# A hybrid decoder layer on one core: a shared PSUM bank and deeper loads in the recurrence, larger key and value weight loads, and two first tiles side by side

## The chip, the cores and the metric

The kernel runs on one core of a Trainium2 chip. The metric is the device time of one execution in microseconds (us). Three executions of the kernel before took 1657.24, 1657.88 and 1666.92 us; their median is 1657.88 us.

## What is computed

One layer of a decoder trunk works on 1024 prompt tokens and 8 x 4 sample tokens (1056 columns in all), with model width 1024 and everything in float32:

```python
h = rmsnorm(x, norm_mix); proj = h @ w_in                # z, xbc, dt, v_pool
xbc = silu(causal_dwconv(conv_buf, xbc))                 # width 4
y = ssd_chunked(xs, dt, a, b_ssm, c_ssm, ssm_h)          # 16 heads, chunks of 128
y = gated_group_rmsnorm(y + xs * ssm_d, z, ssm_norm)
pooled = (window means 2/4/8/16 of v_pool - v_pool) @ w_pool * pool_scale
x = x + concat(y, pooled) @ w_out
k, v = rmsnorm(mem, norm_memkv) @ w_mk, ... @ w_mv       # 256 memory tokens
x = x + attention(rmsnorm(x) @ w_mq, k, v) @ w_mo        # 4 heads
x = x + (silu(g) * val) @ w_down                         # from conv3(rmsnorm(x) @ w_up)
y = rmsnorm(x, final_norm)
```

The prompt's recurrence runs chunk by chunk: for each chunk and head, `exp` of differences of cumulated decays masks `C B^T`, that mask is multiplied with `x dt`, and the state of 128 x 64 is carried on. States, convolution rows, keys and values are outputs too.

## The kernel before, in words

**Tiles.** Activations lie transposed, 128 channels by 1056 tokens. Each float32 product is made of three TensorE products: operands are split into a rounded part (`wh`, `hh`) by ScalarE and a remainder (`wl`, `hl`) by VectorE. `mm_full` (L353) makes one output tile of 128 x 1056 in three PSUM banks: for each of 8 blocks k of 128 channels it issues nine matmuls of 352 columns (three for `wh` with `hh`, three for `wh` with `hl`, three for `wl` with `hh`).

**Weights.** A table of `steps` holds, in the order of use, one unit of 512 weight columns each (256 KB); a unit serves four blocks k. `plains` (L224) enters a unit with a load two steps earlier (`AHEAD`), into the pool `wr` of three buffers, and `wsplit` makes `wh` and `wl` of it (three buffers each). `next_unit` (L299) keeps two units ready ahead of the matmuls.

**Pools.** `stile` gives one of 32 large SBUF tiles (`s`), `ldtile` one of three (`ld`), `mstile` one of two small PSUM banks (`ms`), `mmtile` one of two groups of three banks (`mm`). A new tile takes a buffer when the last user of the old one is done.

**Order.** In the first stage the program's order holds on each engine; later a scheduler orders the instructions of each engine when the kernel is built, and each engine works its list in order. SyncE (SP) issues all loads and stores but a few, also in list order: one that waits holds back those behind it. Generators run beside the matmuls and are advanced by `tick`, one call per block k.

**Start** (L461 to L500, L664 to L672). TensorE first multiplies zeros (`WARM` = 6 instructions, two records each in the trace). `x` arrives in eight blocks `xs[k]`, each split by `x_split(k)` into `hh[k]` and `hl[k]`; the first comes in three pieces. Then two projection tiles are made one after the other, and a third while the norm is found.

**Recurrence** (`ssd_all`, L881). There are 32 units: two groups of heads, eight chunks, two halves of four heads. `ssd_load` (L708) loads 256 KB of cumulated decays (`scr_acs`) into an `s` tile, two units ahead. `ssd_pre` (L715) transposes two blocks of `x` into an `ms` bank, from which VectorE makes `xd`; then ScalarE and VectorE turn the decays into `am` and `ce` in the same `s` tile. `ssd_post` (L741), one unit later, multiplies: the output `py` in one `ms` bank, the new state `pst` in another; VectorE adds both away. All of this lies between the matmuls of the projection tiles.

**Keys and values** (L1060 to L1088). After the pooled half of the output projection (L1047, eight tiles, for each of which `xT` is loaded into an `ld` tile, added and stored), the keys take 8 x 8 blocks of three matmuls of 256 columns, the values 2 x 8 blocks of six matmuls of 512 columns, so that a unit of 256 KB lasts for 12 or for 6 matmuls. The weights `w_mk` and `w_mv` come as 32 such units.

Of the kernel before, what the change touches and what calls it, by code (L numbers as in the profile page):

```python
# [10 lines left out]
ALU = mybir.AluOpType  # L11
# [3 lines left out]
P = 128  # L15
D = 1024
KT = 8
# [6 lines left out]
BW = 352  # L24
TW = 1191
NB = 3
# [2 lines left out]
DFF = 2816  # L29
NJ = DFF // P  # L30
EPS = 1e-6
WARM = 6
XN_TICK = 18
XN_LAG = 6
MEM_EVERY = 1.5
# [1 line left out]
VZ = "ppzppzpzpzpzpzzz"  # L37
SSD_EVERY = 3
SSD_PACE = 1.6
SAMPLE_EVERY = 1.5  # L40
GATE_EVERY = 1.5
FOLD_EVERY = 1.2
WINDOWS = (2, 4, 8, 16)
AHEAD = 2
# [19 lines left out]
XBC_ORDER = (8, 10, 0, 1, 2, 3, 9, 11, 4, 5, 6, 7)  # L64
# [15 lines left out]
def body(ctx, tc, A):  # L80
# [20 lines left out]
    V, S, G, PE, DQ = [InOrder(e) for e in (nc.vector, nc.scalar, nc.gpsimd, nc.tensor, nc.sync)]  # L101
# [3 lines left out]
    def dma(out, in_, after=None):  # L105
        d = DQ.dma_start(out, in_)
        after = after or gate[0]
        if after is not None:
            tc.add_manual_dep(d.ins, after.name, NOSYNC, reason="load order")
        return d  # L110
# [32 lines left out]
    def stile(dt=F32, w=T):  # L143
        return sp.tile([P, w], dt, tag="S", name="s")
# [4 lines left out]
    def ldtile():  # L149
        return lp.tile([P, T], F32, tag="ld", name="ld")  # L150

    def mmtile():
        return pmm[0].tile([P, NB, 512], F32, tag="mm", name="mm")
# [4 lines left out]
    def mstile():  # L158
        if pmm[1] is None:
            return mbtile()  # L160
        return pmm[1].tile([P, 512], F32, tag="ms", name="ms")
# [15 lines left out]
    steps, sources, issue = [], [], {}  # L177
    ready = deque()
    raws = {}
    at = [0]  # L180
# [8 lines left out]
    def load(i):  # L189
        if i in raws:  # L190
            return
        src, alloc = sources[i]
        raw = alloc()
        w = 1
        for d in src.shape[1:]:
            w *= d
        dst = raw[:, :w]
        dma(dst if len(src.shape) == 2 else dst.rearrange("p (k o) -> p k o", k=src.shape[1]), src)
        raws[i] = (raw, w)

    def source(src, step, ahead, alloc=wtile):
        sources.append((src, alloc))
        issue.setdefault(max(0, step - ahead), []).append(len(sources) - 1)
        return len(sources) - 1
# [8 lines left out]
    def wsplit(raw, w):  # L213
        hi = wp.tile([P, 512], F32R, tag="wh", name="wh")
        S.activation(hi[:, :w], raw[:, :w], AF.Copy)
        lo = wp.tile([P, 512], F32R, tag="wl", name="wl")
        V.tensor_tensor(lo[:, :w], raw[:, :w], hi[:, :w].bitcast(F32), op=ALU.subtract)
        ready.append((hi, lo, w))
# [5 lines left out]
    def plains(srcs):  # L224
        for src in srcs:
            i = source(src, len(steps), AHEAD)
            steps.append(lambda i=i: plain(i))

    def up_part(j, n):
        return A["w_up"][2 * j + 2 - int(n[1]), int(n[2]) - 1]  # L230

# [41 lines left out]
    def down_weights(name, m, c):  # L273
        kind = {"t3": 0, "b22": 1, "t1": 2, "t2": 3}
        if name in kind:
# [1 line left out]
        h, r = {"b11": (0, 0), "t4": (1, 1)}[name]  # L277
        return A["w_dn"][h, 4 * r + m][:, c]

    plains(A["w_in"][m, h] for m in range(28) for h in range(2))  # L280
    plains(scr["wop"][4 * h:4 * h + 4, :, m * P:(m + 1) * P].rearrange("k p o -> p k o")
           for m in range(8) for h in range(2))
    plains(A["w_mk"][m][:, h * 512:(h + 1) * 512] for m in range(8) for h in range(2))
    plains(A["w_mv"][4 * d + k // 2][:, (k % 2) * 512:(k % 2) * 512 + 512] for d in range(2) for k in range(8))
    for nm, n in (("w_out_y", 8), ("w_mq", 8), ("w_mo", 8), ("w_mo", 8), ("w_mo", 7)):
        plains(A[nm][m, h] for m in range(n) for h in range(2))
    plains(up_part(j, "a12") for j in EARLY)
# [11 lines left out]
    def next_unit():  # L299
        while len(ready) < 2 and at[0] < len(steps):  # L300
            prep()
        return ready.popleft()
# [14 lines left out]
    def tick():  # L317
        for hk in list(hooks):
            hk[0] -= 1
            if hk[0] <= 0:  # L320
                hooks.remove(hk)
                hk[1]()
        for bs in (bgs, bgs2):
            if bs:
                b = bs[0]
                b[1] += 1
                while b[1] >= b[2]:
                    b[1] -= b[2]
                    if next(b[0], 0) == 0:
                        bs.pop(0)  # L330
                        break
# [21 lines left out]
    def mm_full(nk, xh, xl):  # L353
        ps = mmtile() if pmm[1] else [mbtile() for _ in range(NB)]
        for k in range(nk):
            whi, wlo = next_block()
            for pi, (w, x) in enumerate(((whi, xh[k]), (whi, xl[k]), (wlo, xh[k]))):
                for b in range(NB):
                    PE.matmul(bank(ps, b)[:, :BW], lhsT=w, rhs=x[:, b * BW:(b + 1) * BW],
                              start=(k == 0 and pi == 0), stop=(k == nk - 1 and pi == 2))  # L360
            tick()
        return ps
# [102 lines left out]
    ps = mstile()  # L465
# [6 lines left out]
    for b in range(NB):  # L472
        c = slice(b * BW, (b + 1) * BW)
        dma(xs[0][:, c], A["xT"][0][:, c])
    for k in range(1, 8):
        dma(xs[k][:, :T], A["xT"][k])
        if k in (2, 4):
            load(k // 2)
    dma(cst, A["cst"][:, :256])
    dma(chist, A["conv_hist"])  # L480
    dma(cst2, A["cst"][:, 256:])
# [3 lines left out]
    hh, hl = [], []  # L485
# [10 lines left out]
    prep()  # L496
    for k in range(8):
        x_split(k)
        if k == 2:
            prep()  # L500

    def x_sq(k):
# [86 lines left out]

    xb = [None] * 12  # L590

    def xbc_raw(f):
        ps = mm_full(KT, hh, hl)
        raw = ttile()
        if xr[1:]:
            normed(raw[:, 3:3 + T], ps)
        else:
            S.activation(v3(raw[:, 3:3 + T]), ps[:, :, :BW], AF.Copy)
        return raw
# [64 lines left out]
    later(10, dt_weights)  # L664
    later(XN_TICK, lambda: xr.append(norm_cols(xs[0], T, D)))
    later(XN_TICK + XN_LAG, x_bc)
    early_raw = [xbc_raw(f) for f in XBC_ORDER[:2]]
    strict[0] = "after"
    background(fold_pool(), FOLD_EVERY)
    ps = mm_full(KT, hh, hl)  # L670
# [7 lines left out]
    ps = mmtile()  # L678
    for k in range(KT):
        for pi, x in enumerate((hh[k], hl[k])):  # L680
            for b in range(NB):
                PE.matmul(ps[:2 * H, b, :BW], lhsT=wd[:, k].rearrange("p s h -> p (s h)"),
                          rhs=x[:, b * BW:(b + 1) * BW], start=(k == 0 and pi == 0), stop=(k == KT - 1 and pi == 1))
# [23 lines left out]

    def ssd_load(c, g, hf):  # L708
        h0 = 8 * g + 4 * hf
        at = stile()  # L710
        dma(at[:, 0:512].rearrange("p (h l) -> p h l", h=4),
            scr["acs"][h0:h0 + 4, c * P:(c + 1) * P].partition_broadcast(P))
        return at
# [27 lines left out]
    def ssd_post(c, g, hf, am, ce, xd, btm):  # L741
        l = slice(c * P, (c + 1) * P)
        h0 = 8 * g + 4 * hf
        py = mstile()
        for i in range(2):
            o = slice(i * P, (i + 1) * P)
            for e in range(2):
                PE.matmul(py[64 * e:64 * e + 64, o], lhsT=xd[:, 0, 2 * i + e], rhs=am[:, 2 * i + e],
                          start=True, stop=(c == 0))
            if c > 0:  # L750
                for e in range(2):
                    hc = (h0 + 2 * i + e) * 64
                    PE.matmul(py[64 * e:64 * e + 64, o], lhsT=hT[:, hc:hc + 64], rhs=ce[:, 2 * i + e],
                              start=False, stop=True)
        pst = mstile()
        PE.matmul(pst[:, :256], lhsT=btm, rhs=xd[:, 1].rearrange("p h d -> p (h d)"), start=True, stop=True)
        for i in range(2):
            x = xb[h0 // 2 + i]
            V.scalar_tensor_tensor(x[:, l], x[:, l], pc("ssm_d", h0 // 2 + i), py[:, i * P:(i + 1) * P],
                                   op0=ALU.mult, op1=ALU.add)  # L760
        hs = hT[:, h0 * 64:h0 * 64 + 256]
        if c == 0:
            V.tensor_copy(hs, pst[:, :256])
        else:
            hv = hs.rearrange("p (h d) -> p h d", h=4)
            V.tensor_tensor(hv, hv, cd_t[:, c, h0:h0 + 4].unsqueeze(2).to_broadcast([P, 4, 64]), op=ALU.mult)
            V.tensor_tensor(hs, hs, pst[:, :256], op=ALU.add)
        if c == 7:
            dma(A["o_ssm_p"][:, h0 * 64:h0 * 64 + 256], hs)

# [108 lines left out]
    units = [(c, g, hf) for g in range(2) for c in range(8) for hf in range(2)]  # L879

    def ssd_all():  # L881
        loads = {}
        loads[0] = ssd_load(*units[0])
        loads[1] = ssd_load(*units[1])
        yield
        yield
        pend = None
        for u, un in enumerate(units):
            if un[2] == 0:
                ssd_group(un[0], un[1])  # L890
                yield
            nxt = ssd_pre(*un, loads.pop(u))
            yield
            if pend is not None:
                ssd_post(*pend[0], *pend[1])
            if u + 2 < len(units):
                loads[u + 2] = ssd_load(*units[u + 2])
            yield
            pend = (un, nxt)
        ssd_post(*pend[0], *pend[1])  # L900
        yield
# [145 lines left out]
    for m in range(8):  # L1047
        ps = mm_full(KT, p2h, p2l)
# [11 lines left out]
    for m in range(8):  # L1060
        ps = mbtile()[:, :256]
        for k in range(8):
            whi, wlo = next_block()
# [9 lines left out]
    for d in range(2):  # L1073
        pv = [mbtile() for _ in range(2)]
        for k in range(8):
            whi, wlo, _ = next_unit()
            for mt in range(2):
                c = slice(mt * P, (mt + 1) * P)
# [920 lines left out]
```

## Time and profile before

| | |
|---|---|
| median of three executions | 1657.88 us |
| the profiled execution, its own time | 1659.16 us |
| its span in the profile | 1657.3 us |
| TensorE matmul busy (PE) | 1633.0 us, 99% |
| TensorE weight loads busy (PEld) | 1556.8 us, 94% |
| VectorE (DVE), ScalarE (ACT) busy | 1213.8 us, 73%; 805.2 us, 49% |
| moved by DMA | 287.42 MB, 173 GB/s on average |
| granted TensorE clock, mean | 0.998 |

PE rows are modelled in their ends, so a PE row can run on over a short wait. The weight loads (PEld) have ends of their own, and a wait that PE hides shows there. All instructions go through one recording helper, so the trace tells them apart by the names of their tiles.

### The profile page before, as it was taken

To read this page: it belongs to the slowest core of one execution; us is meant where nothing else is said; L and a number is where in the kernel's file an instruction comes from. 1 tells how busy PE (TensorE), PEld (TensorE's weight loads), DVE (VectorE), ACT (ScalarE), POOL (GpSimd) and SP (SyncE) were. 2 spreads that over 40 slices of the span, in tenths; PEclk is the share of its full clock that TensorE was granted. 3 is DMA by queue.
4 is the path that set the end of the run, shared out by engine and by line. 5 is a ranking of instruction groups with operands and counts; after the bars stand their busy time and mean duration, and the time that the engine had idled before them with its cause. 6 is when DMAs were issued, how large, how long until landed. Compare 5 with 4: busy or idle time off the path is not lost.

```text
span 1657.3 us, 30394 instructions
## 1 busy us (share of the span) xinstructions
PE 1633.0 (99%) x11808; PEld 1556.8 (94%) x11808; DVE 1213.8 (73%) x2044; ACT 805.2 (49%) x1578; POOL 51.5 (3%) x117
## 2 busy tenths in 40 slices
PE   9999999999999999999999999999999999999998
PEld 8899999899989989999888999999999999999997
DVE  7766778688679576754654887888888898866665
ACT  7565643443505342312543666566665656554451
POOL 0110000000000000000000000010000000000000
PEclk9999999999999999999999999999999999999999
DMA  6243354544687578962665654554434356986542
GB/s 222 86 158 92 65 136 105 109 94 100 202 294 269 177 242 302 312 214 72 230 216 191 219 184 120 171 139 119 137 126 146 125 163 196 317 294 191 164 131 105
DMA packets 174592, 287.42 MB, mean 173 GB/s; under 512 B 39936, under 2 KB 77664, under 8 KB 174448
## 3 DMA queue, kind: packets, MB, share of 16 engines
q1 hardware_dynamic: 171584, 281.03, 53.9%
q0 software_dynamic: 2864, 4.46, 1.9%
q8 instruction: 92, 1.51, 0.4%
q14 instruction: 52, 0.43, 0.1%
HBM read 207.89 MB, written 77.53 MB: 172 GB/s over the span
## 4 chain that ended last, share of the span: by engine, by line
PE 74%; DMA 6%; DVE 4%; ACT 1%; issue 1%; SPq 0%; DVEq 0%; ACTq 0%
PE mb L92 59%; PE mm L92 12%; PE ms L92 3%; DMA s<-scr_acs 2%; DVE s L92 2%; DMA q<-scr_g 1%; DVE wl L92 1%; ACT s L92 1%; DMA wr<-w_mk 1%; DMA wr<-w_mo 1%; DVE t L92 0%; DMA scr_pool<-t 0%; DMA ld<-scr_pool 0%; ACT wh L92 0%; DMA wr<-w_up 0%
## 5 line engine op out<-in xcount | busy, mean ns | idle before, releaser
L92 PE MATMUL mb<-s,wh 128*128 128x264 f32 (+4 forms) x4800 | 904.6, 294 | 5.1 <-ACT wh L92 5.1
L92 PEld LDWEIGHTS mb<-s,wh 128*128 128x128 f32 x4800 | 758.4, 189 | 11.9 <-ACT wh L92 6.2
L92 PE MATMUL mb<-s,wl 128*128 128x264 f32 (+4 forms) x2400 | 664.3, 294 | 2.4 <-DVE wl L92 2.3
L92 PEld LDWEIGHTS mb<-s,wl 128*128 128x128 f32 x2400 | 445.4, 189 | 6.9 <-DVE wl L92 4.1
L92 ACT ACTIVATE wh<-wr 128x512 fp32r<-128x512 f32 (+1 forms) x298 | 184.1, 619 | 389.7 <-PE mb L92 181.3
L92 PE MATMUL mm<-s,wh 128*128 128x352 f32 x1728 | 340.8, 330 | 1.0 <-DVE s L92 0.9
L92 PEld LDWEIGHTS mm<-s,wh 128*128 128x128 f32 x1728 | 284.8, 188 | 7.2 <-DVE s L92 2.1
L92 DVE TENSOR_TENSOR wl<-wr,wh 128x512 fp32r<-128x512 f32 (+1 forms) x298 | 201.6, 679 | 112.9 <-ACT wh L92 111.5
L92 PE MATMUL mm<-s,wl 128*128 128x352 f32 x864 | 187.8, 324 | 0.0
L92 DVE SCALAR_TENSOR_TENSOR t<-t,par 128x1104 f32<-128x1104 f32 (+1 forms) x124 | 168.9, 1366 | 19.3 <-ACT t L92 18.5
L92 PEld LDWEIGHTS mm<-s,wl 128*128 128x128 f32 x864 | 147.2, 189 | 1.8 <-issue 1.2
L92 ACT ACTIVATE s<-s 128x512 f32<-128x512 f32 (+7 forms) x117 | 84.2, 731 | 93.4 <-DMA s<-scr_acs 57.4
L92 DVE TENSOR_TENSOR t<-t 128x1024 f32<-128x1024 f32 (+10 forms) x147 | 105.7, 731 | 12.9 <-DMA t<-w_dn 9.7
L92 ACT ACTIVATE wh<-ws 128x512 fp32r<-128x512 f32 x110 | 68.9, 628 | 69.9 <-PE mb L92 67.8
L92 DVE TENSOR_TENSOR s<-s 128x512 f32<-128x512 f32 (+8 forms) x90 | 74.6, 844 | 30.8 <-ACT s L92 30.4
L92 DVE TENSOR_TENSOR wl<-ws,wh 128x512 fp32r<-128x512 f32 x110 | 75.7, 689 | 22.0 <-ACT wh L92 21.7
L92 DVE TENSOR_TENSOR s<-mb,s 128x264 f32<-128x264 f32 (+6 forms) x140 | 61.0, 473 | 31.2 <-PE mb L92 16.3
L92 ACT ACTIVATE t<-mb 128x264 f32<-128x264 f32 (+1 forms) x136 | 53.3, 393 | 57.4 <-PE mb L92 50.3
L92 DVE TENSOR_TENSOR s<-q,s 128x528 fp32r<-128x528 f32 x81 | 56.4, 708 | 25.6 <-ACT s L92 25.4
L92 ACT ACTIVATE t<-t,par 128x1104 f32<-128x1104 f32 (+1 forms) x56 | 73.0, 1304 | 2.3 <-DVE t L92 1.7
L92 ACT ACTIVATE s<-q 128x528 fp32r<-128x528 f32 x81 | 51.9, 643 | 43.0 <-DMA q<-scr_g 41.3
L92 PE MATMUL mb<-s 128*128 128x256 f32 (+2 forms) x414 | 68.8, 323 | 0.0
(195 smaller groups left out, 1427.4 us busy)
## 6 DMA issues: line engine op xcount, KB each, us to landing
q<-scr_g SPq DMA_DIRECT2D x77, 264.0 KB, 4.0
wr<-w_up SPq DMA_DIRECT2D x59, 256.0 KB, 2.9
wr<-w_in SPq DMA_DIRECT2D x56, 256.0 KB, 2.9
wr<-w_mo SPq DMA_DIRECT2D x46, 256.0 KB, 2.8
scr_g<-t SPq DMA_DIRECT2D x22, 528.0 KB, 2.7
ws<-w_up SPq DMA_DIRECT2D x44, 256.0 KB, 2.8
s<-scr_acs SPq DMA_DIRECT2D x33, 256.0 KB, 5.0
t<-w_dn SPq DMA_DIRECT2D x32, 256.0 KB, 4.4
```

What stands on the lines that cost most here:

```text
L92: i = fn(*args, **kwargs)
```

## The change

Four edits are made. (1) `WARM` becomes 3, the two first projection tiles are made side by side for the first four blocks k, and the second tile's first weights are loaded and split earlier. (2) In the recurrence the state `pst` is written to the free half of `py`'s bank. (3) The decays are loaded four units ahead, every second unit into an `ld` tile. (4) The key and value weights are loaded as 16 tiles of 512 KB into `ld` tiles, four steps ahead, and each is split in two halves.

```diff
-WARM = 6
+WARM = 3
+SSD_AHEAD = 4
...
+    def halves(src):
+        i = source(src, len(steps), 2 * AHEAD, ldtile)
+
+        def half(h):
+            load(i)
+            wsplit(raws[i][0][:, h * 512:(h + 1) * 512], 512)
+
+        steps.extend([lambda: half(0), lambda: half(1)])
...
-    plains(A["w_in"][m, h] for m in range(28) for h in range(2))
+    plains(A["w_in"][m, h] for m, h in ((0, 0), (1, 0), (0, 1), (1, 1)))
+    plains(A["w_in"][m, h] for m in range(2, 28) for h in range(2))
...
-    plains(A["w_mk"][m][:, h * 512:(h + 1) * 512] for m in range(8) for h in range(2))
-    plains(A["w_mv"][4 * d + k // 2][:, (k % 2) * 512:(k % 2) * 512 + 512] for d in range(2) for k in range(8))
+    for src in (*(A["w_mk"][m] for m in range(8)), *(A["w_mv"][k] for k in range(8))):
+        halves(src)
...
     for k in range(1, 8):
+        if k in (1, 3):
+            load((k + 1) // 2)
         dma(xs[k][:, :T], A["xT"][k])
-        if k in (2, 4):
-            load(k // 2)
...
         x_split(k)
-        if k == 2:
+        if k in (0, 4):
             prep()
...
+    def two_tiles():
+        ps = [mmtile(), mmtile()]
+        u = [next_unit(), next_unit()]
+        for i, k in [(i, k) for k in range(4) for i in range(2)] + [(i, k) for i in range(2) for k in range(4, 8)]:
+            if k == 4:
+                u[i] = next_unit()
+            whi, wlo, _ = u[i]
+            wc = slice(k % 4 * P, (k % 4 + 1) * P)
+            for pi, (w, x) in enumerate(((whi, hh[k]), (whi, hl[k]), (wlo, hh[k]))):
+                for b in range(NB):
+                    PE.matmul(ps[i][:, b, :BW], lhsT=w[:, wc], rhs=x[:, b * BW:(b + 1) * BW],
+                              start=(k == 0 and pi == 0), stop=(k == 7 and pi == 2))
+            tick()
+            if k == 7:
+                yield ps[i]
...
-    early_raw = [xbc_raw(f) for f in XBC_ORDER[:2]]
+    early_raw = [xbc_raw(f, ps) for f, ps in zip(XBC_ORDER[:2], two_tiles())]
...
-        at = stile()
+        at = ldtile() if (2 * c + hf) % 2 else stile()
...
-        pst = mstile()
-        PE.matmul(pst[:, :256], lhsT=btm, rhs=xd[:, 1].rearrange("p h d -> p (h d)"), start=True, stop=True)
+        pst = py[:, 256:]
+        PE.matmul(pst, lhsT=btm, rhs=xd[:, 1].rearrange("p h d -> p (h d)"), start=True, stop=True)
...
-        loads[0] = ssd_load(*units[0])
-        loads[1] = ssd_load(*units[1])
+        for u in range(SSD_AHEAD):
+            loads[u] = ssd_load(*units[u])
...
-            if u + 2 < len(units):
-                loads[u + 2] = ssd_load(*units[u + 2])
+            if u + SSD_AHEAD < len(units):
+                loads[u + SSD_AHEAD] = ssd_load(*units[u + SSD_AHEAD])
```

In the lists below, numbers behind a name tell one buffer's use from another's. TensorE's list at the start stands before as follows (`s_146`, `s_154`, `s_158` are `hh[0]`, `hh[1]`, `hh[2]`, the numbers one higher `hl`; `wh_142` is the first unit of weights):

```order
L92 MATMUL ms_105<-warm_96 128x512 x6
L92 MATMUL mm_189<-s_146,wh_142 128x352 x3
L92 MATMUL mm_189<-s_147,wh_142 128x352 x3
L92 MATMUL mm_189<-s_146,wl_144 128x352 x3
L92 MATMUL mm_189<-s_154,wh_142 128x352 x3
L92 MATMUL mm_189<-s_155,wh_142 128x352 x3
L92 MATMUL mm_189<-s_154,wl_144 128x352 x3
L92 MATMUL mm_189<-s_158,wh_142 128x352 x3
```

and in the change so (`s_143`, `s_157` are `hh[0]`, `hh[1]`; `mm_192` is the first tile, `mm_193` the second):

```order
L93 MATMUL ms_105<-warm_96 128x512 x3
L93 MATMUL mm_192<-s_143,wh_139 128x352 x3
L93 MATMUL mm_192<-s_144,wh_139 128x352 x3
L93 MATMUL mm_192<-s_143,wl_141 128x352 x3
L93 MATMUL mm_193<-s_143,wh_151 128x352 x3
L93 MATMUL mm_193<-s_144,wh_151 128x352 x3
L93 MATMUL mm_193<-s_143,wl_153 128x352 x3
L93 MATMUL mm_192<-s_157,wh_139 128x352 x3
```

Each block of `x` now serves nine matmuls of either tile before the next block is needed. In the recurrence TensorE's list has, around the end of one unit, before:

```order
L92 MATMUL ms_2141<-s_1882,xd_2017 64x128 x2
L92 MATMUL ms_2141<-s_1882,s_1157 64x128 x2
L92 MATMUL ms_2141<-s_1882,xd_2017 64x128 x2
L92 MATMUL ms_2141<-s_1882,s_1157 64x128 x2
L92 MATMUL ms_2150<-xd_2017,btm_1938 128x256
L92 MATMUL mm_2094<-s_168,wh_1999 128x352 x3
```

and now:

```order
L93 MATMUL ms_2137<-ld_1625,xd_2014 64x128 x2
L93 MATMUL ms_2137<-ld_1625,s_1154 64x128 x2
L93 MATMUL ms_2137<-ld_1625,xd_2014 64x128 x2
L93 MATMUL ms_2137<-ld_1625,s_1154 64x128 x2
L93 MATMUL ms_2137<-xd_2014,btm_1936 128x256
L93 MATMUL mm_2090<-s_165,wh_2091 128x352 x3
```

The state's matmul (`btm`) wrote a bank of its own, `ms_2150`; it now writes that of the output, `ms_2137`, and the decays lie in an `ld` tile. VectorE's list where the last pooled output tile ends and the keys begin stands in the change so (`ld_5233` is the first 512 KB of `w_mk`, `ld_5347` the second; `ld_5498` holds `xT` for the last tile):

```order
L93 TENSOR_TENSOR wl_5510<-ld_5233,wh_5508 128x512
L93 TENSOR_TENSOR ld_5498<-mm_5399,ld_5498 128x1056
L93 TENSOR_TENSOR wl_5532<-ld_5347,wh_5530 128x512
L93 TENSOR_TENSOR wl_5553<-ld_5347,wh_5551 128x512
L93 TENSOR_TENSOR t_5548<-mb_5507,rmb_4490 128x256
```

`ld_5498` takes the buffer of `ld_5233`, so its load waits for the first row here, and the second row waits for that load; before, `xT` was loaded there without such a tie. Behind the keys and values the lists of all engines are the same as before, row for row, but for line numbers and buffer numbers.

## Rows read from the trace of the kernel before

**Rows 1.** Three stretches: us, then busy us of PE, PEld, DVE, ACT, POOL, clock, DMA, GB/s.
```profile
8.26:33.12 24.86, 24.43 (x147) 23.32 (x145) 19.58 (x19) 19.38 (x21) 0.70 (x3) 1.00 0.74 266
205.00:420.00 215.00, 210.13 (x1531) 196.29 (x1530) 166.06 (x355) 87.69 (x158) 5.55 (x18) 1.00 0.50 109
550.95:603.64 52.69, 49.92 (x309) 42.49 (x308) 35.60 (x59) 24.41 (x38) 0.00 (x0) 1.00 0.63 198
```
**Rows 2.** Timeline of TensorE at the start: start, us, what, count, idle before.
```profile
5.07 0.34 PEld L92 LDWEIGHTS ms<-warm 128*128 128x128 f32 x1 [0.52 <-issue]
5.68 0.19 PEld L92 LDWEIGHTS ms<-warm 128*128 128x128 f32 x1 [0.28 <-issue]
8.26 0.19 PEld L92 LDWEIGHTS mm<-s,wh 128*128 128x128 f32 x1 [0.24 <-issue]
...
28.76 1.13 PE L92 MATMUL mm<-s,wh 128*128 128x352 f32 x6
...
33.12 1.13 PE L92 MATMUL mm<-s,wh 128*128 128x352 f32 x6
```
**Rows 3.** Timeline of ScalarE and VectorE at the start: the splits of x.
```profile
6.55 0.59 ACT L92 ACTIVATE s<-s,par 128x352 fp32r<-128x352 f32 x1 [0.73 <-DMA s<-xT]
7.17 0.58 DVE L92 SCALAR_TENSOR_TENSOR s<-s,par 128x352 fp32r<-128x352 f32 x1 [0.73 <-ACT s L92]
8.31 1.18 ACT L92 ACTIVATE s<-s,par 128x1056 fp32r<-128x1056 f32 x1 [1.17 <-DMA s<-xT]
9.52 2.66 DVE L92 SCALAR_TENSOR_TENSOR s<-s,par 128x1056 fp32r<-128x1056 f32 x2 [1.76 <-ACT s L92]
```
**Rows 4.** Waits of PE, PEld, ACT, SP, 205 to 420: us, times, longest.
```profile
PE ms L92 <- DVE xd L92: 4.3, 6, 1.4
PEld ms L92 <- DVE xd L92: 5.9, 7, 1.6
ACT s L92 <- DMA s<-scr_acs: 59.0, 23, 4.9
SPq L92 <- PE ms L92: 39.2, 20, 3.4
```
**Rows 5.** The chain of waits around one unit: start, us, what.
```profile
292.42 6.17 DMA s<-scr_acs
...
300.63 0.70 PE ms L92 x2
```
**Rows 6.** Waits of PEld, 550 to 604, keys and values.
```profile
PEld mb L92 <- DVE wl L92: 3.7, 8, 1.0
PEld mb L92 <- ACT wh L92: 2.7, 3, 1.4
```
**Rows 7.** Timeline of TensorE, unhindered pieces of keys, transposes and values.
```profile
551.35 0.28 PE L92 MATMUL mb<-s,wl 128*128 128x256 f32 x1
...
561.01 0.28 PE L92 MATMUL mb<-s,wl 128*128 128x256 f32 x1
...
588.83 1.20 PE L92 MATMUL mb<-cst,nr 128*128 128x128 f32 x9
...
591.92 0.39 PE L92 MATMUL mb<-wl,s 128*128 128x512 f32 x1
592.62 0.39 PE L92 MATMUL mb<-wl,s 128*128 128x512 f32 x1
```
**Rows 8.** Timeline: a late weight load, and VectorE's other work late in the values.
```profile
561.81 1.97 ACT L92 ACTIVATE wh<-wr 128x512 fp32r<-128x512 f32 x3 [2.76 <-DMA wr<-w_mk]
...
597.74 1.29 DVE L92 TENSOR_TENSOR wl<-wr,wh 128x512 fp32r<-128x512 f32 x2
598.48 0.19 PEld L92 LDWEIGHTS mb<-wl,s 128*128 128x128 f32 x1 [1.00 <-DVE wl L92]
```
**Rows 9.** DMA issues by line: count, KB each, median us to landing.
```profile
wr<-w_mk SPq DMA_DIRECT2D x16, 256.0 KB, 3.2
ld<-xT SPq DMA_DIRECT2D x8, 528.0 KB, 4.9
```

More of the change, by code (lines that the diff above doesn't have):

```diff
@@ L590, in body, with xbc_raw @@
     xb = [None] * 12
-    def xbc_raw(f):
-        ps = mm_full(KT, hh, hl)
+    def two_tiles():
[13 more added lines that the diff above has]
+                yield ps[i]
+    def xbc_raw(f, ps=None):
+        ps = ps or mm_full(KT, hh, hl)
         raw = ttile()
@@ L762, in ssd_post @@
         if c == 0:
-            V.tensor_copy(hs, pst[:, :256])
+            V.tensor_copy(hs, pst)
         else:
@@ L766, in ssd_post @@
             V.tensor_tensor(hv, hv, cd_t[:, c, h0:h0 + 4].unsqueeze(2).to_broadcast([P, 4, 64]), op=ALU.mult)
-            V.tensor_tensor(hs, hs, pst[:, :256], op=ALU.add)
+            V.tensor_tensor(hs, hs, pst, op=ALU.add)
         if c == 7:
```

## The prediction

> **What bounds the kernel now.** I first read the three stretches that the change touches [rows 1]: TensorE is busy for nearly all of each, at a clock granted in full, while VectorE, ScalarE and the DMA queues have room. So TensorE sets the time, and only what it idles can be won: a transfer or a split that becomes quicker counts as far as TensorE waits for it. Next come the waits of TensorE and of its weight loads in each stretch [rows 4, 6], since a PE row can run on over a short wait and a PEld row cannot; then the timelines around those waits for what came late [rows 2, 3, 8], and the chain of waits for the recurrence [rows 5]. Behind the values the lists of all engines are the same as before, so a gain made ahead of them is carried to the end unchanged if nothing there depends on absolute times; I count it in full.
>
> **The start.** Two tiles take 16 groups of nine matmuls. Unhindered, three groups take 33.12 - 28.76 = 4.36 us, 1.45 each [rows 2], so 16 take 23.2. They took 24.86 us [rows 1], from 8.26: 1.6 us of waiting for x, behind a warm-up that ended late. The warm-up's records stand 0.86 us apart up to 5.68, and from there 0.43 apart [rows 2]. Half of its twelve records go; the six that are left end at about 5.7. The first tile can begin there but needs the last third of `hh[0]` at 6.55 + 0.59 = 7.14 and of `hl[0]` at 7.17 + 0.58 = 7.75 [rows 3]. Four more matmuls (0.16 each) end the first group at about 8.4. The second group, the second tile's, needs its weights. Their load now stands right behind the first block of x; it is half as large as the second block of x, which took from 6.5 to 8.3 to come in [rows 3], so I estimate that it lands 0.8 us after 6.5; both splits (0.65 each, as in [rows 8]) are done at 8.6 to 8.8, before its last three matmuls want the remainder, so the second group ends at 9.9. The second block of x comes 0.8 us later than before, at 9.1; its parts take 1.18 on ScalarE and 1.33 on VectorE [rows 3], so `hh[1]` is there at 10.3 and `hl[1]` at 11.6. The third group thus ends at 11.6 + 6 x 0.16 = 12.6. After that each block of x feeds 2.9 us of matmuls and VectorE needs 1.33 for one, so nothing waits: 13 groups x 1.45 bring the third tile's start to 31.4 instead of 33.12. That is **-1.7 us**. Bounds: with no wait but the first, 8.4 + 15 x 1.45 = 30.2, so -2.9; if x comes one block later than I think (1.7 us), 0.
>
> **The recurrence.** ScalarE waited for decays 23 times, 59.0 us in all [rows 4]. The chain shows how that reached TensorE [rows 5]: the load issued at 292.42 took 6.17 us, ScalarE and VectorE came after, and the state's matmul started at 300.63. That matmul needed an `ms` bank which the transposes held until VectorE had made `xd`, and in VectorE's list `xd` stood behind the late decays. Two edits hit the same wait: the state no longer takes a bank, and the loads go out four units ahead. A unit lasts about 215 / 32 = 6.7 us by the stretch [rows 1] (it holds a few units less, so rather more); two more units are over 13 us against a landing of about 6. TensorE waited 4.3 us for `xd`, its weight loads 5.9 [rows 4]. I take **-4.5 us**, near the PE row, because seven waits of PEld hold the short pause that stands before every state matmul as well. Bounds: -5.9 and, if half of the waits move to the next use of a bank, -2. ScalarE, busy 87.69 of 215 us, covers two more table loads that the new order brings. The `ld` tiles were idle here but for early loads of the sample's state and of `pooled`, which now go out after the last decays; they are needed only behind 425 us.
>
> **Keys and values.** Unhindered, a block of the keys takes (561.01 - 551.35) / 27 = 0.358 us and 64 take 22.9; three value matmuls take 592.62 - 591.92 = 0.70, and 32 such triples 22.4; two sets of transposes for a norm take 1.2 each [rows 7]. Sum 47.7, against 52.69 [rows 1]: 5.0 us lost. The waits of PEld say 6.4 [rows 6], the PE row 2.8 (52.69 - 49.92). Most of it are late weights: a load of 256 KB lands after 3.2 us [rows 9], plus two splits of 0.65, and three buffers of 1.43 us each (four blocks) last 4.3 us, which is no reserve; ScalarE waited 2.76 us for one [rows 8]. With 512 KB tiles three buffers last 8.6 us. The nearest row for such a load is `xT` with 528 KB, 4.9 us [rows 9]; with the splits 6.2, so about 2 us of reserve. Two losses stay. Late in the values VectorE has the gate's work in front of the remainders: a wait of 1.0 us at 598.48 has no load behind it but VectorE's own list [rows 8]; I leave 1.1 us for this. And at the seam to the keys `xT` for the last tile can be loaded only when the first 512 KB are split, in mid tile: that is about 5.8 (half a tile) + 1.3 + 4.9 = 12.0 us after the tile's start, while TensorE ends it at 11.6. VectorE then adds it (about 1.3) and splits the next half unit at about 14.0; TensorE wants that after two units, at 14.5. That holds narrowly, and the fourth 512 KB, behind the store in SP's list, come about 0.5 us late. So 5.0 - 1.1 - 0.5: **-3.4 us**. Bounds: -5.0, and 0 if the seam eats it up. Sixteen issues fewer cost SP less; it waits anyway.
>
> **Sum.** -1.7 - 4.5 - 3.4 = -9.6 us. The profiled execution took 1659.16 us, so its like would take 1649.6; the median lies 1.3 below the profiled time, so I predict a median of **1648.3 us**, 0.6% less. A change of under 1% (16.6 us) is what a measurement of this kernel can hardly tell from none: its own three runs lie 0.6% apart.
>
> **Rivals.**
> *The seam starves the keys* (0.15). The three `ld` buffers now serve x, the keys' weights and the stores of `scr_xp`. If the load of the last `xT` takes 8 us instead of 4.9, VectorE stands still in front of it, the next remainders come 3 us late, and the whole reserve of the following loads starts from there. The gain of 3.4 is gone: 1651.7. For it: one list, one blocked row. Against it: the DMA share of the stretch was 0.63 [rows 1].
> *The clock* (0.07). TensorE ran its first records at 0.86 us and later ones at 0.43 [rows 2], the 1.2 and 2.4 GHz levels, having been at work since its first one. With half of the warm-up gone, real work starts just after the rise and has gaps until 11.6. If the clock fell back in them, the groups up to 12.6 would take 2.9 us instead of 1.45; two of them lie on the path, so +2.9 and the start gains nothing: 1650 to 1651. The Trainium skill, "TensorE: Matmul & The Clock Gate", section "Why this matters for your kernels", speaks against this edit, since it advises to warm the engine with matmuls before work that is measured; by it the sum would be the one just given. The rows decide otherwise as far as they go: the rise stands at 5.68, before the shortened warm-up ends.
> *The shared bank makes VectorE late* (0.06). VectorE reads the output from the bank that the state's matmul now writes, so it starts after that matmul, at most 0.70 us later [rows 5], in each of 32 units. Where VectorE is what TensorE waits for, at seven places [rows 4], up to 4.9 us come back: 1653.2; more only if VectorE, busy 166.06 of 215 us [rows 1], were at its limit. The Trainium skill, "PSUM — Partial Sum Buffer", section "PSUM bank collisions raise a hardware error", states the rule behind it: engines must be kept apart by bank and quadrant, not by address. No row of before shows it.
> *The loads do not go out earlier* (0.06). An `s` buffer is still free only when the unit two `s` units back is done. Then the wait for decays stays, and only the bank's part is won: about half, 1650.5.
> *SP holds back the weights* (0.03; slower). SP works its list in order, and a load of decays waits in it for a buffer that TensorE frees. SP already waited 39.2 us for that, at most 3.4 at once [rows 4]. If the four outstanding loads make it stand longer, the weight loads behind it come late. The splits are two units of weights ahead of the matmuls, each 4 x 1.45 = 5.8 us, so it decides from about 12 us at one stand; if 12 of 24 loads went 2 us over it, the gain of the recurrence would turn into 24 us: 1677. The longest wait is far from it.
> *More than I count* (0.05): waits that PE rows hide, all three bounds at once, -13.8, and something behind: 1640 to 1644.
>
> **Numbers.** The forecast itself has 0.58, and lies between 1645 and 1652. With the rivals on either side the range for 8 times in 10 is **1643.5 to 1654.5**. Faster by over 1% needs less than 1641.3: 0.04. Slower by over 1%: the SP rival, 0.03. Within 1%: 0.93.
>
> **What the changed profile would show.** Start: the third tile's first matmul at about 31.4, records at 0.43 from the sixth on. Recurrence: no TensorE wait for `xd` above 0.5 us, ScalarE's wait for `scr_acs` under 10 us. Keys and values: about 49 us from their first matmul to the first of the next product, ScalarE hardly waiting for `w_mk` and `w_mv`. Wrong I would be through a wait at the seam, in SP's list, or late in the values that is longer than before.

## The result and the profile after

The changed kernel takes **1646.59 us** (median of four runs, 1644.07 to 1649.91); the kernel before, run beside it, 1660.79 us (1657.24 to 1666.92). The ratio is **0.9912**, 95% interval 0.9893 to 0.9931. Measured twice more, the change took 1645.43 us, ratio 0.9901 [0.9869, 0.9933], and 1646.34 us, 0.9892 [0.9873, 0.9911]; the kernel before had medians of 1662.10 (25 runs) and 1662.86 us (17 runs) beside it. So the change is worth 14 to 17 us where I said 9.6, and the time came out 1.7 to 2.9 us below the forecast of 1648.3: the gain was larger than I thought, and so was the time it is taken from.

The profiled execution took 1645.04 us, its span is 1642.9, against 1657.3 before. Four matmuls of TensorE's timeline cut the span into stretches; they are, in order, the third tile's first, the first output of the recurrence, the first of the keys, and the first of the next product (start, length, what):

```profile
32.44 1.13 PE L93 MATMUL mm<-s,wh 128*128 128x352 f32 x6
...
160.43 0.66 PE L93 MATMUL ms<-s,xd 128*64 128x128 f32 x8
...
544.94 0.40 PE L93 MATMUL mb<-s,wh 128*128 128x256 f32 x2
...
592.00 1.13 PE L93 MATMUL mb<-s,wh 128*128 128x352 f32 x6
```

Before, the first is at 33.12 [rows 2]; the others are, in the same view of the kernel before:

```profile
161.08 0.66 PE L92 MATMUL ms<-s,xd 128*64 128x128 f32 x8
...
551.11 0.40 PE L92 MATMUL mb<-s,wh 128*128 128x256 f32 x2
...
603.64 1.13 PE L92 MATMUL mb<-s,wh 128*128 128x352 f32 x6
```

The start is 0.7 us shorter, the stretch with the recurrence 390.0 - 384.5 = 5.5, keys and values 52.5 - 47.1 = 5.5, and what follows 1053.7 - 1050.9 = 2.8, though its lists are the same: 14.4 in all. The stretches of [rows 1], in the same view after (us, then busy us of PE, PEld, DVE, ACT, POOL, granted clock, DMA share, GB/s):

```profile
5.69:32.44 26.75, 24.83 (x146) 23.28 (x145) 21.00 (x22) 20.46 (x23) 2.18 (x3) 1.00 0.78 286
205.00:420.00 215.00, 214.34 (x1564) 201.33 (x1563) 164.10 (x350) 80.93 (x145) 5.57 (x18) 1.00 0.49 112
544.94:592.00 47.06, 47.06 (x308) 42.81 (x307) 36.35 (x59) 24.35 (x39) 0.00 (x0) 1.00 0.70 224
```

TensorE is now busy in all of the last and nearly all of the second; the clock is granted in full throughout, as before. The waits that answer to [rows 4, 6] (us in total, times, longest; the first five from 205 to 420, the others in keys and values):

```profile
PE ms L93 <- DVE xd L93: 0.7, 1, 0.7
PEld ms L93 <- DVE xd L93: 1.4, 3, 0.9
ACT ld L93 <- DMA ld<-scr_acs: 44.4, 11, 4.9
ACT s L93 <- DMA s<-scr_acs: 21.7, 10, 3.5
SPq L93 <- PE ms L93: 57.6, 21, 4.3
...
PEld mb L93 <- issue: 0.2, 1, 0.2
ACT wh L93 <- DMA ld<-w_mk: 1.5, 1, 1.5
```

The reader is to see two things: TensorE's waits are gone, and ScalarE's waits for decays are not. They were 59.0 us and are 66.1.

### The profile page after: what moved, and what is told of

It is laid out like the page before. It is cut to its first block, busy times and chain, and to the rows that moved or that the text cites. A ratio compares the mean times of both kernels' runs of the same rounds, so it can differ in the third digit from the quotient of the medians.

```text
span 1642.9 us, 30318 instructions
## 1 busy us (share of the span) xinstructions
PE 1624.7 (99%) x11802; PEld 1553.6 (95%) x11802; DVE 1214.1 (74%) x2044; ACT 806.9 (49%) x1580; POOL 54.2 (3%) x117
## 4 chain that ended last, share of the span: by engine, by line
PE 89%; DMA 5%; DVE 4%; ACT 1%; issue 1%; SPq 0%; ACTq 0%; DVEq 0%
PE mb L93 60%; PE mm L93 22%; PE ms L93 6%; DVE s L93 2%; DMA q<-scr_g 2%; DVE wl L93 1%; ACT s L93 1%; DMA ld<-scr_pool 1%; DVE t L93 0%; DMA s<-xT 0%; SPq L93 0%; DMA ld<-scr_acs 0%; DMA t<-scr_z 0%; DMA ld<-h0T 0%; DMA wr<-scr_dn 0%
## 5 line engine op out<-in xcount | busy, mean ns | idle before, releaser
L93 ACT ACTIVATE wh<-wr 128x512 fp32r<-128x512 f32 (+1 forms) x266 | 164.2, 618 | 365.6 <-PE mb L93 170.1
L93 DVE TENSOR_TENSOR wl<-wr,wh 128x512 fp32r<-128x512 f32 (+1 forms) x266 | 178.8, 673 | 103.0 <-ACT wh L93 101.4
L93 ACT ACTIVATE s<-s 128x512 f32<-128x512 f32 (+7 forms) x87 | 65.1, 764 | 31.4 <-DMA s<-scr_acs 21.7
L93 DVE TENSOR_TENSOR s<-s 128x528 fp32r<-128x528 f32 (+8 forms) x76 | 64.5, 867 | 6.8 <-ACT s L93 6.3
```

The source lines that it names most:

```text
L93: i = fn(*args, **kwargs)
```

## Experiments

Medians are compared only between kernels that were measured together, on one chip and beside the same runs of the kernel before. One profile shows one execution, so I also read the same stretches from all fourteen. "Units" is the time from the first to the last state matmul (`btm`) of the 32 units of the recurrence, "keys" the time from the first key matmul to the first of the next product, "rest" from there to the end of the span; us:

```
kernel                       third tile  units   keys   rest
before                          33.12    253.7   52.5   1053.7
e3 loads of 512 KB alone        34.08    258.3   47.1   1052.0
e7 short warm-up alone          33.59    257.6   51.0   1052.0
f2 start alone                  32.28    258.0   51.4   1053.3
e2 four units ahead alone       34.11    256.6   53.0   1049.1
e1 shared bank alone            33.80    250.5   51.7   1052.7
f1 change, two units ahead      32.25    251.5   47.1   1052.8
change (after, e4, f3)    31.58..32.44   248.0..248.4   47.1..47.5   1050.9..1053.3
e8 change, 256 KB loads         31.48    249.1   47.1   1052.7
e5 change, x earlier            30.86    249.2   47.1   1053.8
e6, f4 change, long warm-up  32.83, 32.27  249.2, 248.0  47.1  1049.2, 1054.0
```

**e1: the shared bank alone**, in the kernel before.

```diff
-        pst = mstile()
+        pst = py[:, 256:]
...
```

> The kernel before with one edit: the state's product is written to the free half of the output's bank; decays are still loaded two units ahead. Measured by the stretch from the first output matmul of the recurrence to the first matmul of the keys, 389.9 us before and 384.5 in the change (5.4 gained). Theory: late decays and the bank that the transposes hold are one wait, and taking the bank away lets TensorE run on into the projection matmuls while xd is late, so most comes from this alone: 385 to 387 us, TensorE's wait for xd under 1.5 us, while ScalarE still waits some 50 us for decays. Rival, the loads carry the gain: 389 to 390 us, the wait moves to the next transposes or outputs. Rival, each edit has its own half: 387 to 388. Whole kernel: 3 to 5 us less than before by the theory, 0 to 1 by the first rival.

1658.26 us (10 runs) against 1662.10, ratio 0.9978 [0.9964, 0.9991]. Its profile is its quickest run (1655.20). The stretch of the theory takes 386.9 us there, within the 385 to 387 expected; the units take 250.5 us, and TensorE's wait for `xd` from 205 to 420 is down to this, a little over the 1.5 expected, while ScalarE still waits 69.5 us for decays:

```profile
PE ms L92 <- DVE xd L92: 1.9, 3, 1.3
```

**e2: four units ahead alone**, in the kernel before.

```diff
+SSD_AHEAD = 4
...
-        at = stile()
+        at = ldtile() if (2 * c + hf) % 2 else stile()
...
```

> The kernel before with one edit: decays loaded four units ahead, every second unit into an ld tile; the state keeps a bank of its own. Theory (one wait, two cures): with the decays on time xd is on time and the bank is free when the state's matmul wants it, so this alone also brings the stretch from 389.9 to 384.5 to 386 us, and ScalarE's wait for decays falls from 59 us to under 15. Rival, the bank carries the gain: 388 to 390 us although ScalarE waits little. Rival, the loads do not go out earlier since s buffers are still freed late: ScalarE still waits over 40 us for decays.

1658.78 us (10 runs), ratio 0.9979 [0.9963, 0.9994]. The theory fell: the waits of the same stretch are no smaller than in the kernel before:

```profile
PE ms L93 <- DVE xd L93: 6.7, 5, 2.4
...
ACT ld L93 <- DMA ld<-scr_acs: 51.3, 11, 5.8
ACT s L93 <- DMA s<-scr_acs: 15.4, 9, 3.6
```

Where the 3.3 us of its median come from, its profile does not show: the units take 256.6 us, as long as in kernels with two units ahead (253.7 to 258.3), and only the rest, which the edit does not touch, is short.

**e3: the 512 KB loads alone**, in the kernel before.

```diff
...
-    plains(A["w_mk"][m][:, h * 512:(h + 1) * 512] ...)
-    plains(A["w_mv"][4 * d + k // 2][:, ...] ...)
+    for src in (*(A["w_mk"][m] for m in range(8)), *(A["w_mv"][k] for k in range(8))):
+        halves(src)
```

> The kernel before with one edit: key and value weights in 512 KB ld tiles four steps ahead. The stretch of keys and values took 52.7 us before and 47.1 in the change. Theory: the gain of 5.6 us is this edit's alone, so 47.0 to 47.6 us here, no wait of the weight loads over 0.5 us, and the whole kernel is 5 to 6 us shorter than before. Rival, part of it comes from the earlier stages (the seam or VectorE's list stands better because of them): 48.5 to 50.5 us.

1657.85 us (10 runs), ratio 0.9975 [0.9962, 0.9988]: 4.2 us less. Keys and values take 47.05 us, as in the whole change, so the theory holds. Its recurrence, that of before, took 4.6 us longer than in the profile of before. One place shows how (e3, timeline of VectorE, then of TensorE):

```profile
221.69 0.69 DVE L92 TENSOR_TENSOR s<-s 128x512 f32<-128x512 f32 x1 [5.36 <-ACT s L92]
222.30 0.68 DVE L92 TENSOR_TENSOR xd<-ms,dtp 128x512 f32<-128x512 f32 x1
...
223.04 0.70 PE L92 MATMUL ms<-xd,btm 128*128 128x256 f32 x2 [2.38 <-DVE xd L92]
```

It is the mechanism of [rows 5]: VectorE stands 5.36 us in front of late decays, `xd` behind them comes late, and the state's matmul waits for the bank. How often and how long differs from profile to profile.

**e4: the change once more**, unaltered.

> The change itself once more, for the scatter of one program. From the first x1 matmul behind the values to the end both programs have the same lists, yet that part took 1053.7 us before and 1050.9 in the change's first profile. Theory: these 2.8 us are scatter of late weight loads, so the same part takes 1050 to 1055 us here, and differs by up to 3 us among this call's four profiles without regard to the edits. Rival, the change shortens the rest too: 1050 to 1051.5 us here and some 1053.5 in the three kernels that lack parts of it.

1645.43 us (four runs), ratio 0.9901 [0.9869, 0.9933]. The rest takes 1051.8 us here and 1052.7, 1049.1 and 1052.0 in e1, e2 and e3: it scatters without regard to the edits, as the theory has it.

**e5: the change, with x earlier.** Of the first two units of weights only the first 128 columns go ahead of x's second block, and of `par` only eight columns ahead of all. The third unit's load and the splits of what is left move back too.

```diff
...
-    dma(par, A["par"])
-    load(0)
+    dma(par[:, :8], A["par"][:, :8])
+    first_load(0, ca)                      # ca: the first 128 columns
...
+        if k == 1:
+            first_load(1, ca)
+        if k == 2:
+            first_load(0, cb)              # cb: the rest
+            first_load(1, cb)
...
```

> The change with a shorter way to the second block of x: of the parameters only the eight columns of the first norm are loaded ahead, and of the first two weight units only the 128 columns of the first block; the rest follows behind the second block of x. That takes some 0.55 MB out of what is ahead of it. Theory: the start is bound by the second block of x (its two splits ended at 11.07 and 12.43 us, and TensorE stood still from 10.0 to 12.5 but for three matmuls), so the third tile begins at 30.8 to 31.5 us instead of 32.44, and the kernel is 1 to 1.6 us shorter than the change. Rival, the weights' splits or the order on VectorE bind next: 32 to 32.5, nothing won.

The third tile starts at 30.86, about 1 us before the change's own (31.58 to 32.44). The time is 1649.95 us (four runs), ratio 0.9912 [0.9883, 0.9940], no better than the change. TensorE waits in e5 (from 36 to 161, and from 420 to 545 us) where the change has waits of at most 0.5:

```profile
PE ms L93 <- DVE nsu L93: 0.8, 1, 0.8
...
PE ms L93 <- DVE rbc L93: 1.5, 1, 1.5
```

The first goes with a real loss: from the third tile to the first output of the recurrence e5 takes 129.25 us, the change (after, e4, f3) 127.98 to 128.02, so the microsecond was given back by 161 us. That the later load of `par` causes it was not tried. The second is not the edit's: e8, which starts as the change does, waits 1.4 us at the same place.

**e6 and f4: the change with the long warm-up**, with one run and with four.

```diff
-WARM = 3
+WARM = 6
```

> The change with the long warm-up of before (six instructions instead of three). Theory: TensorE waits for the second block of x in any case, so starting at 8.3 instead of 5.7 costs nothing: the third tile begins at 32.3 to 32.6 as in the change (32.44). Rival, the warm-up is what the start gained: 33.1 or later.

> The change with the whole warm-up of before (six instead of three matmuls). Theory: the first real matmul comes at 8.3 instead of 5.7, the wait for x's second block is hidden behind it, and the third tile starts about 1 us later (32.6 to 33.0), so the median is about 1 us above that of the change. Rival: the third tile's start is set by x's arrival alone, which the warm-up doesn't touch; then there is no difference, and half a warm-up was no part of the gain.

e6 took 1644.97 us (one run); f4 1645.83 us (four runs) beside 1646.34 of the change, ratios 0.9891 and 0.9892 to the kernel before. The third tile starts at 32.83 and 32.27. 32.83 lies in the range of f4's theory, 32.27 on its rival's side, and the medians differ by 0.5 us, the long warm-up being the faster. So the shorter warm-up shows no gain, as f4's rival has it; but the 1 us of the theory is less than the intervals, some 3 us to either side, can tell.

**e7: the short warm-up alone**, in the kernel before.

> The kernel before with the short warm-up and nothing else. Theory: one tile takes 1.45 us for each block of x, which comes every 1.4 us, so it waits for x to the last block and the third tile begins at 32.7 to 33.2 us (33.12 before). Rival, the warm-up is what the start gained: 32.4 or earlier. Rival, the clock falls back in the gaps: 34 us or later, and matmuls of 352 columns at about twice their 0.16 us.

1660.13 us (one run) beside 1663.22; the third tile at 33.59 is later than the 32.7 to 33.2 expected and lies within the 33.12 to 34.11 of the kernels with the start of before. The rival of the clock does not show either: behind the longest idle time, 0.93 us, three matmuls take 0.76 us, in the change 0.75.

**e8: the change, but each 512 KB tile filled by two loads of 256 KB.**

```diff
...
+            dma(dst[:, :512], src[:, :512])
+            dma(dst[:, 512:], src[:, 512:])
...
```

> The change with each 512 KB tile of key and value weights filled by two loads of 256 KB, issued one behind the other. Theory: the gain of the keys and values comes from six half units of buffer in place of three, not from larger transfers, so the stretch stays at 47.0 to 47.6 us. Rival, larger transfers and sixteen issues fewer carry it: 49 us or more, with waits for w_mk or w_mv on ScalarE.

1648.46 us (one run). Keys and values take 47.05 us, as with whole loads. Loads of keys and values in e8 and in the change (count, KB each, median us to landing):

```profile
ld<-w_mv SPq DMA_DIRECT2D x16, 256.0 KB, 3.6
ld<-w_mk SPq DMA_DIRECT2D x12, 256.0 KB, 3.5
```
```profile
ld<-w_mv SPq DMA_DIRECT2D x8, 512.0 KB, 4.0
ld<-w_mk SPq DMA_DIRECT2D x6, 512.0 KB, 4.4
ld<-xT SPq DMA_DIRECT2D x1, 528.0 KB, 3.3
```

What counts is that three tiles of 512 KB stand ready instead of three of 256 KB, not the size of a load. The larger tiles and the longer lead (four steps instead of two) were not tried apart.

**f1: the change without the four units ahead.** After e2 I held the loads ahead for worthless.

```diff
-SSD_AHEAD = 4
+SSD_AHEAD = 2
...
-        at = ldtile() if (2 * c + hf) % 2 else stile()
+        at = stile()
```

> The change without its loads four units ahead: the decays go out two units ahead, all into s tiles, as before; the shared bank, the two tiles side by side and the 512 KB loads stay. Theory: the shared bank alone won the recurrence, and the multiplications by the decays moved forward in VectorE's list together with their loads, so nothing waits less. Then the stretch from the first output matmul of the recurrence to the first key matmul takes 385 to 388 us as in the whole change, and the median is within 2 us of that of the change in this call. Rival: the loads ahead are worth the 3.3 us by which the kernel with them alone lay below the kernel before. Then the stretch takes about 389 us and the median is 3 us above that of the change.

1651.85 us (six runs), ratio 0.9927 [0.9911, 0.9942], beside 1646.34 and 0.9892 of the change: 5.5 us. The stretch of the theory takes 388.2 us, in the change (f3) 384.1. My theory fell, and the rival had even too small a price. The waits for `xd` of TensorE and its weight loads (205 to 420 us) and VectorE's longest (165 to 420), of f1 and then of the change beside it (f3):

```profile
PE ms L93 <- DVE xd L93: 2.8, 3, 1.5
PEld ms L93 <- DVE xd L93: 4.2, 5, 1.7
...
DVE s L93 <- ACT s L93: 43.7, 21, 4.7
```
```profile
PE ms L93 <- DVE xd L93: 0.3, 1, 0.3
PEld ms L93 <- DVE xd L93: 0.8, 2, 0.6
...
DVE ld L93 <- ACT ld L93: 23.1, 8, 4.4
```

With two units ahead VectorE waits for decays 21 times, with four 8 times in the units whose decays lie in `ld` tiles, and twice, 1.2 us, in the others. ScalarE's own wait for decays is the same in both, 70.1 and 71.7 us (165 to 420). The sum of the unit spacings falls from 251.5 to 248.0 us, the even pace of 8.0 and 7.6 us in turn that every profile with both edits shows, but for one unit in some. The profile of f1 is its quickest run (1650.34), so 3.5 is what it shows of 5.5.

**f2: the start alone**, in the kernel before (all edits to the first two tiles, and the short warm-up).

> The kernel before with the start of the change alone: three matmuls of warm-up, weights of the first two units loaded early, two tiles side by side. Theory: it is worth what the third tile's first matmul shows between kernels with and without it, about 1.9 us (31.5 to 32.4 against 33.1 to 34.1), so a ratio of 0.999 to the kernel before. Rival: the parts tried alone gave 3.6, 3.3 and 4.1 us, the whole change 15 to 16; if parts simply add, the start has to give the other 4 to 5 us, ratio 0.997, and it would have to show behind the third tile.

1661.20 us (12 runs) against 1662.86, ratio 0.9982 [0.9969, 0.9995]. The interval holds the theory's 0.999 and the rival's 0.997; the profile speaks for the theory, with the third tile at 32.28 and no gain behind it. What part of it the side-by-side order and the earlier weights have was not tried apart. By the medians the parts alone give 3.8 (e1), 3.3 (e2), 4.2 (e3) and 1.7 us (f2), 13.0 in all, and the loads ahead give 5.5 instead of 3.3 once the bank is shared; that makes 15.2 of the 16.5. Each of these parts is uncertain by about 2 us to either side, so whether they simply add is not shown.

**f3: the change, beside f1, f2 and f4.**

> The change itself, timed in the same call as the other three. Every theory expects 1645 to 1648 us and a ratio of 0.990 to 0.992. Its profile shows the scatter of the stretches: third tile's first matmul at 31.4 to 32.5, recurrence to first key matmul 384 to 387 us, keys and values 47.0 to 47.6 us, from there to the end 1049 to 1054 us.

1646.34 us (five runs), ratio 0.9892 [0.9873, 0.9911]; all stretches as expected.

## Why the prediction was right or wrong

**The start (-1.7): right, as a mean.** The profile after shows only 0.7, but both sides scatter. The four profiles with the old start (before, e1, e2, e3) have the third tile at 33.12 to 34.11, mean 33.8; the six with the new one (after, e4, e8, f1, f2, f3) at 31.48 to 32.44, mean 32.0: 1.8 us, and f2's medians say 1.7. Where the profile after lost its 1.0 against my 31.4, its timelines show (ScalarE, VectorE, TensorE; the last bracket is the idle time before and what ended it):

```profile
9.89 1.18 ACT L93 ACTIVATE s<-s,par 128x1056 fp32r<-128x1056 f32 x1 [2.17 <-DMA s<-xT]
...
11.10 2.66 DVE L93 SCALAR_TENSOR_TENSOR s<-s,par 128x1056 fp32r<-128x1056 f32 x2 [2.65 <-ACT s L93]
...
11.12 0.75 PE L93 MATMUL mm<-s,wh 128*128 128x352 f32 x3 [1.08 <-ACT s L93]
12.47 0.75 PE L93 MATMUL mm<-s,wh 128*128 128x352 f32 x3 [0.60 <-DVE s L93]
```

x's second block came at 9.89 where I had 9.1; `hh[1]` and `hl[1]`, and the two waits that I placed in front of them, follow from it, and nothing waits after. Half of this term's story was idle: as far as f4 and e7 can tell, the warm-up could have stayed as it was.

**The recurrence (-4.5): right mechanism, too small.** In the two profiles the units take 253.7 and 248.4 us, 5.3 less. But the kernel before was lucky there: three other profiles with its recurrence (e3, e7, f2) take 257.6 to 258.3; in e7 and f2 all engines have the same lists in that stretch. The mean of the four is 256.9, that of the seven with both edits (after, e4, f3, e5, e6, e8, f4) 248.5: 8.4 us. The step that failed is that I read the term, and its bound of 5.9, off the waits of one execution. A wait that hangs on when a load lands differs from run to run, and the edit takes away the bad runs too.

That no wait for `xd` would be above 0.5 us is nearly so: there is one of 0.7, and one of 1.3 to 1.5 in e5, e6 and e8. That ScalarE would wait under 10 us for decays was wrong. In the change a load goes out 46.7 us before its unit's state matmul instead of 23.9 (medians of the 11th to 30th unit), but ScalarE's and VectorE's work on it moved forward in their lists as well, so both still stand in front of loads in flight (after; ScalarE, VectorE, TensorE):

```profile
297.42 0.63 ACT L93 ACTIVATE ld<-ld 128x512 f32<-128x512 f32 x1 [4.13 <-DMA ld<-scr_acs]
...
298.09 0.69 DVE L93 TENSOR_TENSOR ld<-ld,s 128x512 f32<-128x512 f32 x1 [4.07 <-ACT ld L93]
298.70 0.68 DVE L93 TENSOR_TENSOR xd<-ms,dtp 128x512 f32<-128x512 f32 x1
...
299.44 0.33 PE L93 MATMUL ms<-cst,s 128*128 128x128 f32 x1 [0.66 <-DVE xd L93]
```

The wait of 4.13 us is no shorter than those of before (59.0 us in 23 times, [rows 4]); what reaches TensorE is 0.66. My rival that the loads do not go out earlier had the sign of ScalarE's wait right, the cause and the conclusion wrong: f1 shows that the loads ahead are worth 5.5 us beside the shared bank. The rival of the bank acts, but at no price: from 165 to 420 us VectorE waits for the state's matmul 12 times, 2.3 us in all, where before it never did, but TensorE's wait for VectorE is down to the 0.7 us shown above.

**Keys and values (-3.4): right mechanism, too small by 1 to 1.5.** Profiles without the new loads take 51.0 to 53.0 us (before, e1, e2, e7, f2; mean 51.9), with them 47.05 to 47.5: 4.4 to 4.9 us on the mean, 5.5 between the two profiles. What was missed is partly in the loss, since the stretch without waits takes 47.05 us where I had 47.7, and partly in the two losses that I left in the sum and that are not there. VectorE's gate work is still in front of the remainders late in the values, but each is done ahead of its first weight load, by 0.3 us at the narrowest and 3.2 at the most, and TensorE's stretch has no wait, neither in the change nor in e3. And at the seam (after; VectorE, then SP's issue of `xT`):

```profile
539.50 0.69 DVE L93 TENSOR_TENSOR wl<-ld,wh 128x512 fp32r<-128x512 f32 x1 [0.38 <-ACT wh L93]
545.14 1.26 DVE L93 TENSOR_TENSOR ld<-mm,ld 128x1056 f32<-128x1056 f32 x1 [4.95 <-PE mm L93]
546.32 0.68 DVE L93 TENSOR_TENSOR wl<-ld,wh 128x512 fp32r<-128x512 f32 x1
```
```profile
540.22 0.33 SPq L93 DMA_DIRECT2D ld<-xT  x1
```

`xT` was asked for at 540.22 and took 3.3 us, not 4.9; VectorE waited for TensorE's tile, not for the load. The rival of the seam had no place to act.

**What follows (0): right, but for scatter.** The 2.8 us behind the values are no gain: over fourteen profiles of one and the same program there the rest takes 1049.1 to 1054.0 us, with no relation to what is ahead of it.

**The clock, and SP's list.** TensorE's weight loads tell its level in the profile after (start, length, what):

```profile
5.07 0.34 PEld L93 LDWEIGHTS ms<-warm 128*128 128x128 f32 x1 [0.52 <-issue]
5.66 0.19 PEld L93 LDWEIGHTS mm<-s,wh 128*128 128x128 f32 x1 [0.26 <-ACT s L93]
...
11.12 0.46 PEld L93 LDWEIGHTS mm<-s,wh 128*128 128x128 f32 x3 [1.37 <-ACT s L93]
```

One takes 0.34 us in the warm-up and 0.19 from 5.66 on, where the rise stands before as well [rows 2]; behind the longest gap three take 0.46, so the engine stayed at the upper level; the clock is granted at 1.00 from 5.69 to 32.44. That row alone would not tell: it says 1.00 from 4.20 to 5.10 too, where the records still stand 0.86 us apart. SP's wait for TensorE's `ms` did become longer, which I had named as a sign of being wrong: 57.6 us and at most 4.3, against 39.2 and 3.4 [rows 4]. It comes with the loads ahead (57.3 in e2, 17.5 in f1), stays far from the 12 us from which I let it count, and between 205 and 420 us no split waits for a load of weights. Neither rival came about.

**The sum.** Corrected by the means over the profiles it reads -1.8 for the start, -8.4 for the recurrence and -4.8 for keys and values: -15.0, against 14 to 17 measured. I also started from a median of 1657.88 us of three runs; with more runs the four medians of the kernel before lie at 1660.8 to 1663.2. The low start of 3 to 5 us and the gain that was 5 to 7 too small partly cancelled: that the forecast came within 3 us was luck in part.

## What to carry to other kernels

A wait that comes from a load landing late is not one number: read it in several executions before pricing its removal, because the one profiled may be a good one. Two edits against the same wait can hide each other: in the profiles the deeper prefetch cut TensorE's wait for `xd` only once the matmul no longer needed the bank that the late work held (2.8 to 0.3 us from f1 to f3, but 6.7 in e2). The times, 5.5 us with the shared bank and 3.3 without, point the same way but lie within their intervals. If work on the prefetched data moves forward in the engines' lists with the load, the waits stay in the profile, and only those of the bounding engine tell whether anything was won.

## What the runs showed that I had not expected

A load of 512 KB landed in 4.0 to 4.4 us, one of 256 KB into the same tiles in 3.5 to 3.6: twice the data for 0.4 to 0.9 us more. In e8 the small loads go out in pairs; in the kernel before those of `w_mk` took 3.2 [rows 9]. And 14.4 us between two profiles can hold 2.8 us of pure scatter in a stretch in which the program did not change.
